# Gate and up as whole 1 MB tiles in the expert steps of four

## Chip, core and metric

The kernel runs on one NeuronCore of a Trainium2 chip. The metric is the device time of one execution in microseconds (us); the median of 3 runs is given. Five engines work side by side: PE (matrix products; its weight loads are listed as PEld), DVE, ACT and POOL (element-wise work), and SP, which here issues nearly all DMAs.

## What is computed

Two pre-norm residual layers on 256 tokens of 1024 channels, all in float32. Layer 0 mixes tokens with a Conformer convolution module, layer 1 with causal differential attention. Each mixer is followed by a mixture of experts, then by a gated per-layer embedding; a final RMSNorm ends the trunk. The part that matters here is the mixture: 32 experts in 4 groups of 8, each token going to one group and to 2 experts in it.

```python
D_MODEL, SEQ, DEPTH = 1024, 256, 2
N_GROUPS, EXPERTS_PER_GROUP, TOP_K_IN_GROUP = 4, 8, 2
D_EXPERT = 256
...
    for g in range(N_GROUPS):
        hg = jnp.einsum("bsd,edf->bsef", h, w_gate[g])
        ug = jnp.einsum("bsd,edf->bsef", h, w_up[g])
        act = jax.nn.silu(hg) * ug * combine[:, :, g, :, None]
        out = out + jnp.einsum("bsef,efd->bsd", act, w_down[g])
```

An expert has three matrices of 1 MB: gate and up are 1024 x 256, down is 256 x 1024. Both layers read all 32 experts, so 192 MB of expert weights pass through the core in one execution.

## The kernel before

Weights go through a ring of 16 slots of 1 MB in SBUF. The class `Stream` holds a list of tiles in the order of their use; `fill` (line 204) takes the next ones, gives each a slot and has SP issue its loads. A slot is freed when `done` (line 233) is called for its tile, and `done` calls `fill` again. The list is therefore the order of the DMA queue: `add_experts` (line 269) writes it for the experts.

A mixture runs in steps, by the table `STEPS` (line 31). Layer 0 has 8 steps of four experts with 32 token slots each. Layer 1 sorts its experts by their counts of tokens: 8 steps of two experts (64 slots each; one of these steps is cut differently) and then 4 steps, 8 to 11, of four experts with 32 slots. In layer 1 the matrices of all places but the first six are found at run time, through `load_found` (line 260).

In every step `add_experts` lists, for `c4` = 0 and 1, one tile per expert that holds half of gate and half of up: of the 8 rows of 256 that each of the 128 partitions owns, four of gate and four of up. Two loads of 512 KB fill it, each 4 KB per partition. After the tiles of both halves come the down tiles, one load of 1 MB each, 8 KB per partition. Three tiles of the first step of each layer (`EARLY`) are loaded ahead into buffers of their own.

The work of a step u in `moe` (line 1024) is, in this order on PE: `gate_up(u, 0, 4)` and `gate_up(u, 4, 8)` (line 1129), `slots(u)` and the token dispatch of a later step, `combine` of the step before, `turn(u)`, and `down(u)` (line 1162). In `gate_up` the tokens of an expert (`hg`) are the stationary operand and the weights stream through:

```python
for c in range(c0, c1):
    for e, s0, width, at in columns(steps[u]):
        ...
        nc.tensor.matmul(ps[at:at + width], hg[:, c, s1:s1 + width], w[:, :, c % 4],
```

With 32 slots per expert, four experts write the four quarters of one PSUM bank: columns 0 to 255 are gate, 256 to 511 are up, and one matmul of 512 columns makes both for one of the 8 rows. PE asks for the four tiles of a half one after the other. `finish_up` (line 1144) turns gate and up into the activation, and after `down(u)` the step's four down slots are freed.

Loads wait at SP in two ways: for the last reader of the slot, and for the semaphore that the load uses. Eight such semaphores go round (DMAHW0 to DMAHW7 in the rows of order below).

Of the kernel before, what the change touches and what calls it, by code (L numbers as in the profile page):

```python
# [32 lines left out]
         + [[(6, 0, 32), (6, 32, 32), (6, 64, 32), (31, 0, 32)]]  # L33
         + [[(7 + 2 * u, 0, 64), (8 + 2 * u, 0, 64)] for u in range(4)]
         + [[(15 + 4 * u + h, 0, 32) for h in range(4)] for u in range(4)])
LAYOUTS = ((0, 32, 64, 96), (0, 64), (0, 96))
CAP = 32
RING = 16
# [51 lines left out]
def kernel(  # L90
# [158 lines left out]
    def places(step):  # L249
        return list(dict.fromkeys(part[0] for part in step))  # L250
# [3 lines left out]
    def expert(e):  # L254

        if e not in order:
            order[e] = nc.sync.value_load(order["row"][0:1, e:e + 1], min_val=0, max_val=NE - 1)
        return bass.ds(order[e] + NE, 1)

    def load_found(t, e, c4):  # L260
        if c4 is None:
            w = moe_w_down.rearrange("l g e f d -> (l g e) f d")[expert(e)]
            nc.sync.dma_start(t, w.rearrange("o (p c) n -> p (o c) n", c=2))
            return
        for m, w in enumerate((moe_w_gate, moe_w_up)):
            w = w.rearrange("l g e d f -> (l g e) d f")[expert(e)].rearrange("o (p c) f -> p (o c) f", c=8)
            nc.sync.dma_start(t[:, 4 * m:4 * m + 4], w[:, 4 * c4:4 * c4 + 4])

    def add_experts(i):
        for u, step in enumerate(STEPS[i]):  # L270
            for c4 in range(2):
                for e in places(step):
                    b = (i * NE + e) * D * F + c4 * 4 * F
                    key = ("gu", i, e, c4)
                    src = [dram(w, b, [[8 * F, P], [F, 4], [1, F]]) for w in (moe_w_gate, moe_w_up)]
                    if i and e >= FIXED:
                        if W.held is None:
                            W.held = len(W.src)
                        src = lambda t, e=e, c4=c4: load_found(t, e, c4)
                    if key[2:] in EARLY[i]:  # L280
                        W.early[key] = src
                    else:
                        W.add(key, src, (8, F))
            if u == PROJ_AT[i]:
                W.add(("proj", i), dram(ple_w_proj, i * 256 * D, [[2 * D, P], [D, 2], [1, D]]), (2, D))
            for e in places(step):
                b = (i * NE + e) * D * F
                src = dram(moe_w_down, b, [[2 * D, P], [D, 2], [1, D]])
                if i and e >= FIXED:
                    src = lambda t, e=e: load_found(t, e, None)  # L290
                W.add(("down", i, e), src, (2, D))

    for jj in range(4):
# [730 lines left out]
    def moe(i, R, between):  # L1024
# [4 lines left out]
        with ExitStack() as ctx:  # L1029
# [99 lines left out]
            def gate_up(u, c0, c1):  # L1129
                hg = hgs[u // 2]  # L1130
                if c0 == 0:
                    gus[u] = ps_a()
                ps = gus[u]
                for c in range(c0, c1):
                    for e, s0, width, at in columns(steps[u]):
                        s1 = (u % 2) * P + at
                        w = W.get("gu", i, e, c // 4).rearrange("p (s c) f -> p s c f", s=2)
                        nc.tensor.matmul(ps[at:at + width], hg[:, c, s1:s1 + width], w[:, :, c % 4],  # L1138
                                         start=(c == 0), stop=(c == 7))
                    if c % 4 == 3:  # L1140
                        for e in places(steps[u]):
                            W.done("gu", i, e, c // 4)

            def finish_up(u):
                ps = gus.pop(u)
# [812 lines left out]
```

## Time and profile before

| | |
|---|---|
| median of 3 runs | 816.93 us (814.59 to 819.43) |
| profiled execution | 815.6 us |
| its span, first to last instruction | 813.9 us |
| PE busy | 699.6 us (86%) |
| PE weight loads busy | 423.5 us (52%) |
| DVE, ACT, POOL busy | 389.4, 297.8, 128.6 us |
| DMA | 246.29 MB in 76112 packets, mean 303 GB/s |
| gate and up matmuls, line 1138 | 191.5 us busy, 50.1 us idle before |
| down matmuls, line 1170 | 82.1 us busy, 9.5 us idle before |

The span is one execution on the chip, as the hardware profiler took it. Busy time is the union of an engine's instructions; a busy PE need not run at its peak. "Idle before" is the time in which the engine waited in front of such an instruction. The DMA share is the mean busy share of the 16 DMA engines of the core and can come out slightly over 1. PE's granted clock has two levels, 1.2 and 2.4 GHz; the page gives it as a share of the higher.

### The profile page before, as it was taken

The numbers are of one execution on the slowest core, as the hardware profiler recorded it, in microseconds if no ns is written. First come the engines' busy times: TensorE is split into PE (matmuls) and PEld (weight loads), VectorE is DVE, ScalarE is ACT, GpSimd is POOL, SyncE is SP. The second block draws the span as 40 slices with busy tenths as digits, with TensorE's granted clock in tenths as the row PEclk, the third lists the DMA queues.
The fourth block names the chain that finished last, engine by engine and source line by source line (L and its number), as shares of the span: only waits on it lengthen the run. The fifth ranks groups of instructions, "written<-read, shape, count | busy, mean of one in ns | idle before, by whom it ended". The sixth has DMA issues, their size and how long they took to land.

```text
span 813.9 us, 11540 instructions
## 1 busy us (share of the span) xinstructions
PE 699.6 (86%) x4038; PEld 423.5 (52%) x4038; DVE 389.4 (48%) x1018; ACT 297.8 (37%) x668; POOL 128.6 (16%) x195
## 2 busy tenths in 40 slices
PE   5999968897786778779999898988999999877796
PEld 3788656643331333225898786764445444422255
DVE  3699975622220521217767886572334324202174
ACT  1577723521110212007656666452212212210064
POOL 1487862000000000001013342100000000000011
PEclk9899989999998989879999999997999999999899
DMA  6990365789999999999854128672899999999951
GB/s 186 337 395 9 89 270 166 282 331 405 411 416 413 409 415 410 413 400 376 264 185 155 54 104 307 249 272 104 332 404 397 412 412 411 412 410 413 416 205 52
DMA packets 76112, 246.29 MB, mean 303 GB/s; under 512 B 8626, under 2 KB 29811, under 8 KB 67602
## 3 DMA queue, kind: packets, MB, share of 16 engines
q1 hardware_dynamic: 75906, 245.24, 78.7%
q8 instruction: 34, 0.56, 0.3%
q10 hardware_dynamic: 144, 0.26, 0.1%
q14 instruction: 28, 0.23, 0.1%
HBM read 244.43 MB, written 1.05 MB: 302 GB/s over the span
## 4 chain that ended last, share of the span: by engine, by line
PE 27%; DMA 12%; DVE 7%; ACT 5%; issue 1%; SPq 0%; POOL 0%; POOLq 0%; ACTq 0%; DVEq 0%
PE psa L1138 7%; DMA wslot<-in_moe_w_up_dram 5%; PE psd L1170 4%; DMA wslot<-in_moe_w_down_dram 4%; PE psb L1076 3%; DMA wslot<-in_ple_w_gate_dram 2%; PE psa L430 2%; DVE wslot L189 2%; PE psa L431 2%; PE psa L432 2%; PE psd L1184 2%; DMA wslot<-in_moe_w_gate_dram 1%; ACT e L1649 1%; ACT wslot L173 1%; PE psc L431 1%
## 5 line engine op out<-in xcount | busy, mean ns | idle before, releaser
L1138 PE MATMUL psa<-wslot,hg 128*32 128x512 f32 (+1 forms) x1008 | 191.5, 675 | 50.1 <-DMA wslot<-in_moe_w_up_dram 49.7
L1138 PEld LDWEIGHTS psa<-wslot,hg 128*32 128x32 f32 (+1 forms) x1008 | 52.5, 127 | 180.1 <-issue 164.2
L1120 DVE TENSOR_REDUCE wc<-psb 32x1 f32<-32x2 f32 (+1 forms) x66 | 10.3, 156 | 208.4 <-PE psb L1115 207.7
L1170 PE MATMUL psd<-wslot,aT 128*32 128x512 f32 (+1 forms) x528 | 82.1, 604 | 9.5 <-DVEq L1404 2.8
L1147 ACT ACTIVATE sg<-psa 128x256 f32<-128x256 f32 x20 | 7.7, 385 | 208.7 <-PE psa L1138 208.7
L1174 DVE TENSOR_TENSOR dl<-psd,dh 128x512 fp32r<-128x512 f32 x40 | 27.6, 692 | 88.4 <-ACT dh L1173 88.4
L872 PE MATMUL psa<-hT,wslot 128*128 128x256 f32 x256 | 58.6, 388 | 1.7 <-DVE hT L761 1.7
L1187 DVE TENSOR_TENSOR x<-x,psd 128x512 f32<-128x512 f32 x80 | 50.0, 683 | 16.1 <-PE psd L1184 16.1
L872 PEld LDWEIGHTS psa<-hT,wslot 128*128 128x128 f32 x256 | 49.7, 195 | 9.3 <-DVE hT L761 2.2
L1170 PEld LDWEIGHTS psd<-wslot,aT 128*32 128x32 f32 (+1 forms) x528 | 21.5, 117 | 59.8 <-issue 45.3
L1173 ACT ACTIVATE dh<-psd 128x512 fp32r<-128x512 f32 x40 | 23.8, 597 | 78.4 <-PE psd L1170 78.4
L387 POOL TENSOR_SCALAR rstd<-ss 128x1 f32<-128x1 f32 x7 | 3.0, 424 | 294.8 <-ACT sq L394 293.9
L821 DVE SCALAR_TENSOR_TENSOR chain<-vp,wT,chain 128x256 f32<-128x256 f32 x119 | 48.0, 483 | 0.2
L1076 PE MATMUL psb<-S,xh 128*128 128x256 f32 x144 | 40.0, 310 | 4.5 <-DVE st L1126 2.2
L430 PE MATMUL psa<-wslot,hTa 128*128 128x256 f32 x144 | 43.5, 302 | 0.0
L1081 ACT ACTIVATE hg<-psb,gains 128x256 f32<-128x256 f32 x72 | 30.3, 471 | 33.5 <-PE psb L1076 33.3
L431 PE MATMUL psa<-wslot,hTa 128*128 128x256 f32 x144 | 41.4, 287 | 0.0
L432 PE MATMUL psa<-wslot,hTa 128*128 128x256 f32 x144 | 41.3, 287 | 0.0
L796 ACT ACTIVATE prod<-vp,wT 128x256 f32<-128x256 f32 x83 | 35.9, 498 | 12.6 <-POOL vp L786 6.8
L1076 PE MATMUL psb<-S,xl 128*128 128x256 f32 x144 | 36.7, 287 | 0.0
L801 POOL TENSOR_TENSOR part<-part,prod 128x256 f32<-128x256 f32 x51 | 35.4, 735 | 0.0
L189 DVE TENSOR_TENSOR wslot<-wslot 128x512 fp32r<-128x512 f32 x39 | 33.4, 885 | 2.7 <-ACT wslot L188 2.7
(344 smaller groups left out, 1340.8 us busy)
## 6 DMA issues: line engine op xcount, KB each, us to landing
wslot<-in_moe_w_down_dram SPq DMA_DIRECT2D x64, 1024.0 KB
wslot<-in_moe_w_gate_dram SPq DMA_DIRECT2D x122, 512.0 KB
wslot<-in_moe_w_up_dram SPq DMA_DIRECT2D x122, 512.0 KB
wslot<-in_conv_w_pw_dram SPq DMA_DIRECT2D x12, 1024.0 KB
wslot<-in_da_w_qkv_dram SPq DMA_DIRECT2D x12, 1024.0 KB
wslot<-in_ple_w_gate_dram SPq DMA_DIRECT2D x8, 1024.0 KB
wslot<-in_da_w_o_dram SPq DMA_DIRECT2D x4, 1024.0 KB
early<-in_moe_w_gate_dram SPq DMA_DIRECT2D x6, 512.0 KB
```

The costliest lines, as they stand in the source:

```text
L189: eng.tensor_tensor(lo, w, hi.bitcast(F32), op=ALU.subtract)
L430: nc.tensor.matmul(ps, h[:, 0, c], wh, start=first, stop=False)
L431: nc.tensor.matmul(ps, h[:, 0, c], wl, start=False, stop=False)
L432: nc.tensor.matmul(ps, h[:, 1, c], wh, start=False, stop=last)
L796: nc.scalar.activation(pr, vps[j][:, k:k + T], AF.Copy, scale=wT[:, j, k:k + 1])
L801: nc.gpsimd.tensor_tensor(part[:, n % 2], part[:, n % 2], pr, op=ALU.add)
L821: nc.vector.scalar_tensor_tensor(pc[n], vps[j][:, k:k + T], wT[:, j, k:k + 1], pe if start else pc[n], op0=ALU.mult, op1=ALU.add)
L872: nc.tensor.matmul(pws[j][:, (1 - half) * T:(2 - half) * T], W.get("pw1", j // 2, 1 - half)[:, c, j % 2 * P:(j % 2 + 1) * P], hT[:, c], st ...
L1076: nc.tensor.matmul(ps[:, c * 256:(c + 1) * 256], xx[tt][:, cc], S[:, tt], start=(n == 0), stop=(n == 3))
L1138: nc.tensor.matmul(ps[at:at + width], hg[:, c, s1:s1 + width], w[:, :, c % 4], start=(c == 0), stop=(c == 7))
L1170: nc.tensor.matmul(pd[at:at + w], aT[:, c, at:at + w], W.get("down", i, e)[:, c, k * 512:(k + 1) * 512], start=(c == 0), stop=(c == 1))
L1187: nc.vector.tensor_add(x[:, tt, ks], x[:, tt, ks], ps)
```

## The change

A table `WHOLE = (1, 8)` names for each layer the first step that is done the new way: steps 1 to 7 of layer 0 and 8 to 11 of layer 1, the steps of four experts but for the first of layer 0. In these, `add_experts` lists the four gate matrices of the step as tiles of their own and then the four up matrices, each with one load of 1 MB that takes 8 KB per partition. `gate_up` reads gate in its first half and up in its second: for all 8 rows and four experts a matmul of 256 columns, into the left and then the right half of the same PSUM bank. `load_found` now takes the list of matrices and the first row. The other steps keep their tiles, loads and matmuls.

```diff
--- before.py
+++ after.py
@@ -33,6 +33,8 @@
          + [[(6, 0, 32), (6, 32, 32), (6, 64, 32), (31, 0, 32)]]
          + [[(7 + 2 * u, 0, 64), (8 + 2 * u, 0, 64)] for u in range(4)]
          + [[(15 + 4 * u + h, 0, 32) for h in range(4)] for u in range(4)])
+
+WHOLE = (1, 8)
 LAYOUTS = ((0, 32, 64, 96), (0, 64), (0, 96))
 CAP = 32
 RING = 16
@@ -257,37 +259,38 @@
             order[e] = nc.sync.value_load(order["row"][0:1, e:e + 1], min_val=0, max_val=NE - 1)
         return bass.ds(order[e] + NE, 1)
 
-    def load_found(t, e, c4):
-        if c4 is None:
-            w = moe_w_down.rearrange("l g e f d -> (l g e) f d")[expert(e)]
-            nc.sync.dma_start(t, w.rearrange("o (p c) n -> p (o c) n", c=2))
-            return
-        for m, w in enumerate((moe_w_gate, moe_w_up)):
-            w = w.rearrange("l g e d f -> (l g e) d f")[expert(e)].rearrange("o (p c) f -> p (o c) f", c=8)
-            nc.sync.dma_start(t[:, 4 * m:4 * m + 4], w[:, 4 * c4:4 * c4 + 4])
+    def load_found(t, e, ws, c0=0):
+        n = t.shape[1] // len(ws)
+        for m, w in enumerate(ws):
+            w = w.rearrange("l g e a b -> (l g e) a b")[expert(e)]
+            w = w.rearrange("o (p c) n -> p (o c) n", c=2 if ws == (moe_w_down,) else 8)
+            nc.sync.dma_start(t[:, m * n:(m + 1) * n], w[:, c0:c0 + n])
 
     def add_experts(i):
         for u, step in enumerate(STEPS[i]):
-            for c4 in range(2):
-                for e in places(step):
-                    b = (i * NE + e) * D * F + c4 * 4 * F
-                    key = ("gu", i, e, c4)
-                    src = [dram(w, b, [[8 * F, P], [F, 4], [1, F]]) for w in (moe_w_gate, moe_w_up)]
-                    if i and e >= FIXED:
-                        if W.held is None:
-                            W.held = len(W.src)
-                        src = lambda t, e=e, c4=c4: load_found(t, e, c4)
-                    if key[2:] in EARLY[i]:
-                        W.early[key] = src
-                    else:
-                        W.add(key, src, (8, F))
+
+            parts = [((w,), 0) for w in (moe_w_gate, moe_w_up)]
+            if u < WHOLE[i]:
+                parts = [((moe_w_gate, moe_w_up), 4 * c4) for c4 in range(2)]
+            for n, e in [(n, e) for n in range(2) for e in places(step)]:
+                ws, c0 = parts[n]
+                b = (i * NE + e) * D * F + c0 * F
+                src = [dram(w, b, [[8 * F, P], [F, 8 // len(ws)], [1, F]]) for w in ws]
+                if i and e >= FIXED:
+                    if W.held is None:
+                        W.held = len(W.src)
+                    src = lambda t, e=e, ws=ws, c0=c0: load_found(t, e, ws, c0)
+                if u == 0 and (e, n) in EARLY[i]:
+                    W.early["gu", i, e, n] = src
+                else:
+                    W.add(("gu", i, e, n), src, (8, F))
             if u == PROJ_AT[i]:
                 W.add(("proj", i), dram(ple_w_proj, i * 256 * D, [[2 * D, P], [D, 2], [1, D]]), (2, D))
             for e in places(step):
                 b = (i * NE + e) * D * F
                 src = dram(moe_w_down, b, [[2 * D, P], [D, 2], [1, D]])
                 if i and e >= FIXED:
-                    src = lambda t, e=e: load_found(t, e, None)
+                    src = lambda t, e=e: load_found(t, e, (moe_w_down,))
                 W.add(("down", i, e), src, (2, D))
 
     for jj in range(4):
@@ -1131,15 +1134,19 @@
                 if c0 == 0:
                     gus[u] = ps_a()
                 ps = gus[u]
-                for c in range(c0, c1):
-                    for e, s0, width, at in columns(steps[u]):
-                        s1 = (u % 2) * P + at
-                        w = W.get("gu", i, e, c // 4).rearrange("p (s c) f -> p s c f", s=2)
-                        nc.tensor.matmul(ps[at:at + width], hg[:, c, s1:s1 + width], w[:, :, c % 4],
-                                         start=(c == 0), stop=(c == 7))
-                    if c % 4 == 3:
-                        for e in places(steps[u]):
-                            W.done("gu", i, e, c // 4)
+                whole = u >= WHOLE[i]
+                for n in range(c0 // 4, c1 // 4):
+                    for c in range(8) if whole else range(4 * n, 4 * n + 4):
+                        for e, s0, width, at in columns(steps[u]):
+                            s1 = (u % 2) * P + at
+                            w, out = W.get("gu", i, e, n), ps[at:at + width]
+                            if whole:
+                                w, out = w[:, c], out[:, n * F:(n + 1) * F]
+                            else:
+                                w = w.rearrange("p (s c) f -> p s c f", s=2)[:, :, c % 4]
+                            nc.tensor.matmul(out, hg[:, c, s1:s1 + width], w, start=(c == 0), stop=(c == 7))
+                    for e in places(steps[u]):
+                        W.done("gu", i, e, n)
 
             def finish_up(u):
                 ps = gus.pop(u)
```

Two engines show what is issued now. PE in step 1 of layer 0, before (psa is the PSUM bank, wslot the ring, hg the tokens; a wait names the semaphore of a load):

```order
L1138 MATMUL psa<-wslot,hg 32x512 [waits DMAHW6_49,DMAHW5_49]
L1138 MATMUL psa<-wslot,hg 32x512 [waits DMAHW7_49,DMAHW0_49]
L1138 MATMUL psa<-wslot,hg 32x512 [waits DMAHW2_49,DMAHW1_49]
L1138 MATMUL psa<-wslot,hg 32x512 [waits DMAHW4_49,DMAHW3_49]
L1138 MATMUL psa<-wslot,hg 32x512 x12
L1138 MATMUL psa<-wslot,hg 32x512 [waits DMAHW6_49,DMAHW5_49]
L1138 MATMUL psa<-wslot,hg 32x512 [waits DMAHW7_49,DMAHW0_49]
L1138 MATMUL psa<-wslot,hg 32x512 [waits DMAHW2_49,DMAHW1_49]
L1138 MATMUL psa<-wslot,hg 32x512 [waits DMAHW4_49,DMAHW3_49]
L1138 MATMUL psa<-wslot,hg 32x512 x12
L1111 MATMUL psb<-wgt_hl,S 128x8 x2
```

and with the change, where each half has four matmuls that wait for one load each, and 28 more of 256 columns:

```order
L1147 MATMUL psa<-wslot,hg 32x256 [waits DMAHW5_49]
L1147 MATMUL psa<-wslot,hg 32x256 [waits DMAHW6_49]
L1147 MATMUL psa<-wslot,hg 32x256 [waits DMAHW7_49]
L1147 MATMUL psa<-wslot,hg 32x256 [waits DMAHW0_49]
L1147 MATMUL psa<-wslot,hg 32x256 x28
L1147 MATMUL psa<-wslot,hg 32x256 [waits DMAHW1_49]
L1147 MATMUL psa<-wslot,hg 32x256 [waits DMAHW2_49]
L1147 MATMUL psa<-wslot,hg 32x256 [waits DMAHW3_49]
L1147 MATMUL psa<-wslot,hg 32x256 [waits DMAHW4_49]
L1147 MATMUL psa<-wslot,hg 32x256 x28
L1114 MATMUL psb<-wgt_hl,S 128x8 x2
```

The first of the half's matmuls for each expert waited for two loads and now waits for one; 12 that follow became 28, half as wide. What stands behind them on PE is the same.

SP in the second half of the same step and its down tiles, before:

```order
L215 DMA wslot<-in_moe_w_gate_dram 128x1024 [waits DMAHW5_49,PE_49]
L215 DMA wslot<-in_moe_w_up_dram 128x1024 [waits DMAHW6_49]
L215 DMA wslot<-in_moe_w_gate_dram 128x1024 [waits DMAHW7_49,PE_49]
L215 DMA wslot<-in_moe_w_up_dram 128x1024 [waits DMAHW0_49]
L215 DMA wslot<-in_moe_w_gate_dram 128x1024 [waits DMAHW1_49,PE_49]
L215 DMA wslot<-in_moe_w_up_dram 128x1024 [waits DMAHW2_49]
L215 DMA wslot<-in_moe_w_gate_dram 128x1024 [waits DMAHW3_49,PE_49]
L215 DMA wslot<-in_moe_w_up_dram 128x1024 [waits DMAHW4_49]
L217 DMA wslot<-in_moe_w_down_dram 128x2048 [waits DMAHW5_49,PE_49]
L217 DMA wslot<-in_moe_w_down_dram 128x2048 [waits DMAHW6_49,PE_49]
L217 DMA wslot<-in_moe_w_down_dram 128x2048 [waits DMAHW7_49,PE_49]
L217 DMA wslot<-in_moe_w_down_dram 128x2048 [waits DMAHW0_49,PE_49]
```

and with the change:

```order
L217 DMA wslot<-in_moe_w_up_dram 128x2048 [waits DMAHW1_49,PE_49]
L217 DMA wslot<-in_moe_w_up_dram 128x2048 [waits DMAHW2_49,PE_49]
L217 DMA wslot<-in_moe_w_up_dram 128x2048 [waits DMAHW3_49,PE_49]
L217 DMA wslot<-in_moe_w_up_dram 128x2048 [waits DMAHW4_49,PE_49]
L219 DMA wslot<-in_moe_w_down_dram 128x2048 [waits DMAHW5_49,PE_49]
L219 DMA wslot<-in_moe_w_down_dram 128x2048 [waits DMAHW6_49,PE_49]
L219 DMA wslot<-in_moe_w_down_dram 128x2048 [waits DMAHW7_49,PE_49]
L219 DMA wslot<-in_moe_w_down_dram 128x2048 [waits DMAHW0_49,PE_49]
```

Eight loads of 128x1024 elements became four of 128x2048, which is the shape that the down loads have, and every load now waits for the slot's last reader itself.

## Rows read from the trace of the kernel before

**Rows 1.** Page, part 2: bytes moved in 40 slices, and the packets.

```profile
GB/s 186 337 395 9 89 270 166 282 331 405 411 416 413 409 415 410 413 400 376 264 185 155 54 104 307 249 272 104 332 404 397 412 412 411 412 410 413 416 205 52
DMA packets 76112, 246.29 MB, mean 303 GB/s; under 512 B 8626, under 2 KB 29811, under 8 KB 67602
```

**Rows 2.** Stretches by stage: us, busy (instructions) by engine, PE clock, DMA share, GB/s.

```profile
174.00:184.00 10.00, 9.76 (x91) 4.12 (x84) 2.84 (x10) 1.82 (x4) 0.00 (x0) 1.00 0.77 244
184.00:214.00 30.00, 25.41 (x171) 10.99 (x173) 8.38 (x18) 5.47 (x12) 0.00 (x0) 0.94 1.02 413
...
640.00:683.00 43.00, 43.00 (x241) 20.85 (x245) 16.50 (x34) 10.80 (x24) 0.00 (x0) 1.00 1.02 413
...
723.00:782.00 59.00, 43.04 (x233) 14.09 (x234) 13.38 (x29) 6.06 (x11) 0.00 (x0) 0.91 1.01 410
```

**Rows 3.** Waits of PE (184:372, then 678:779): us, times, longest.

```profile
PE psa L1138 <- DMA wslot<-in_moe_w_up_dram: 37.5, 27, 1.6
...
PE psa L1138 <- DMA wslot<-in_moe_w_up_dram: 12.3, 9, 1.5
```

**Rows 4.** Timeline of PE, layer 1: step 10, and the end of step 11.

```profile
723.14 3.63 PE L1138 MATMUL psa<-wslot,hg 128*32 128x512 f32 x28 [0.46 <-DMA wslot<-in_moe_w_up_dram]
...
764.62 3.59 PE L1138 MATMUL psa<-wslot,hg 128*32 128x512 f32 x26 [1.53 <-DMA wslot<-in_moe_w_up_dram]
...
774.50 3.62 PE L1170 MATMUL psd<-wslot,aT 128*32 128x512 f32 x26 [1.46 <-DMA wslot<-in_moe_w_down_dram]
```

**Rows 5.** Page, part 6: loads of expert weights, count and KB each.

```profile
wslot<-in_moe_w_down_dram SPq DMA_DIRECT2D x64, 1024.0 KB
wslot<-in_moe_w_gate_dram SPq DMA_DIRECT2D x122, 512.0 KB
```

**Rows 6.** Timeline of PE, layer 0, step 4: start, us, what.

```profile
247.39 1.02 PE L1138 MATMUL psa<-wslot,hg 128*32 128x512 f32 x2 [1.53 <-DMA wslot<-in_moe_w_up_dram]
249.94 1.02 PE L1138 MATMUL psa<-wslot,hg 128*32 128x512 f32 x2 [1.53 <-DMA wslot<-in_moe_w_up_dram]
```

**Rows 7.** Stretches with gate and up loads alone (columns of Rows 2).

```profile
212.00:227.00 15.00, 10.55 (x58) 2.47 (x52) 1.45 (x3) 1.19 (x2) 0.00 (x0) 0.80 1.03 409
...
306.00:321.00 15.00, 14.96 (x82) 5.73 (x82) 1.62 (x3) 3.85 (x7) 0.00 (x0) 1.00 1.03 408
```

**Rows 8.** Stretches with down loads alone (columns of Rows 2).

```profile
201.00:207.00 6.00, 6.00 (x36) 1.92 (x33) 0.39 (x3) 0.38 (x1) 0.00 (x0) 0.75 1.02 423
232.00:238.00 6.00, 5.44 (x41) 2.64 (x42) 1.44 (x7) 0.78 (x3) 0.00 (x0) 1.00 1.02 424
...
327.00:332.00 5.00, 4.66 (x26) 1.26 (x26) 0.00 (x0) 0.00 (x0) 0.00 (x0) 0.68 1.01 419
357.00:361.00 4.00, 3.24 (x16) 0.92 (x20) 0.00 (x0) 0.00 (x0) 0.00 (x0) 0.57 1.01 418
```

**Rows 9.** Timeline of PE, layer 0: step 1, and the end of step 7.

```profile
174.39 7.05 PE L1138 MATMUL psa<-wslot,hg 128*32 128x512 f32 x64
...
357.76 5.18 PE L1138 MATMUL psa<-wslot,hg 128*32 128x512 f32 x26 [1.51 <-DMA wslot<-in_moe_w_up_dram]
```

**Rows 10.** Stretches where layer 1's queue fills again (columns of Rows 2).

```profile
572.00:578.00 6.00, 6.00 (x30) 1.95 (x26) 0.34 (x1) 0.12 (x1) 0.00 (x0) 1.00 0.80 283
578.00:584.00 6.00, 6.00 (x38) 4.32 (x39) 4.34 (x10) 2.33 (x6) 0.00 (x0) 1.00 1.02 424
```

**Rows 11.** Chain of waits: start, us, what (a load, issue to landing).

```profile
744.04 10.22 DMA wslot<-in_moe_w_up_dram
```

**Rows 12.** Timeline of PE's weight loads: step 3, and the end of step 7.

```profile
233.17 0.16 PEld L1138 LDWEIGHTS psa<-wslot,hg 128*32 128x32 f32 x4 [0.27 <-issue]
233.60 0.16 PEld L1138 LDWEIGHTS psa<-wslot,hg 128*32 128x32 f32 x4 [0.27 <-issue]
...
367.72 0.16 PEld L1170 LDWEIGHTS psd<-wslot,aT 128*32 128x32 f32 x8 [0.99 <-DMA wslot<-in_moe_w_down_dram]
```

**Rows 13.** Groups by line: busy us, mean ns of one (convolution).

```profile
L872 PE MATMUL psa<-hT,wslot 128*128 128x256 f32 x256 | 58.6, 388 | 1.7 <-DVE hT L761 1.7
```

## The prediction

> **What bounds the kernel now.** I read the slices of the span first. The moved bytes stand at 400 GB/s and more in two long stretches, and mostly far lower elsewhere [rows 1]. The stage table puts numbers on that: from 184 us on (layer 0's experts) and from 640 to 782 us (layer 1's) the 16 DMA engines are busy all the time (share 1.01 to 1.02) at 410 to 413 GB/s, while PE has gaps [rows 2]. So in both stretches the weights come as fast as the DMA engines carry them, and PE waits: 37.5 us for up tiles between 184 and 372 us, 12.3 us between 678 and 779 us [rows 3]. Up to 723 us PE in layer 1 runs without such a wait (the one of 0.46 us there is the first [rows 4]); that does not contradict it, since the DMA engines are full at the same time, and it is they that are still behind when PE has caught up.
>
> Next, what the engines carry. The issue part of the page has 64 down loads of 1 MB and 122 gate loads of 512 KB [rows 5]; beside each gate load stands one of up. A down load takes 8 KB from one place for each of 128 partitions, a half gate or up load 4 KB. The packet line says the same: 76112 packets, 67602 of them under 8 KB, and the remaining 8510 are close to 66 x 128 = 8448, the down loads and the two of the projection [rows 1]. So one row is one packet, and the trace already holds both sizes.
>
> Do they run at different speeds? I picked stretches in which only one kind is in flight. Where PE is released by one up tile after another, 2.55 us apart, it is gate and up, as from 247.39 to 249.94 us [rows 6]. The ten microseconds after a step's last up tile are down. Two stretches of the first kind ran at 409 and 408 GB/s, mean 408.5 [rows 7]; four of the second at 418 to 424, mean 421 [rows 8]. The DMA share is full in all six. A tile of 1 MB so costs 1048.6/408.5 = 2.567 us in 4 KB rows and 1048.6/421 = 2.491 us in 8 KB rows: **0.076 us less**. From the slower end of one to the slower end of the other (409 to 418) it is 0.055, from 408 to 424 it is 0.097.
>
> **The change, part by part.** *Loads.* Seven steps of layer 0 (1 to 7) and four of layer 1 (8 to 11) load eight 1 MB tiles of one matrix each, so 88 tiles go from two loads with 4 KB rows to one with 8 KB rows, the shape of the down loads. The bytes and the order (8 tiles, then 4 down) stay.
> - Step 1 of layer 0, 8 tiles: worth nothing. PE ran its gate and up at 174.39 us in one piece of 64 records (the trace has two for a matmul) without a wait [rows 9]; the tiles had been there.
> - Steps 2 to 7, 48 tiles: 48 x 0.076 = 3.6 us (2.6 to 4.7).
> - Layer 1, 32 tiles: 32 x 0.076 = 2.4 us. The first eight travel while PE still works without waiting [rows 4]; if they only come earlier into slots that PE frees no sooner, 24 count: 1.8 us. Ends 1.3 and 3.1.
> - The start of step 2. Between 174 and 184 us, where the queue fills again, 4 KB rows ran at only 244 GB/s [rows 2]. Layer 1 has the same: 283 GB/s from 572 to 578 us on 4 KB rows, then 424 as soon as 8 KB rows follow [rows 10]. Were step 2's tiles at 421 here, 10 x (1 - 244/421) = 4.2 us would be gained; if the slowness belongs to the filling of the queue, nothing. No row shows 8 KB rows in those first microseconds, so I take a quarter, 1.0 us.
>
> *SP.* 88 issues go. SP is not what is waited for, since it runs ahead: a load issued at 744.04 us took 10.22 us to land [rows 11], four tiles of 2.55 us, so eight loads are in flight. With 1 MB each that is 8 MB and some 20 us ahead. The ring has 16 slots and PE holds the four of the current half, so slots suffice, and what stands behind (routing inputs, projection, gate weights of the stage after) keeps its place in bytes. Zero.
>
> *PE.* 32 more matmuls in each of the 11 steps, each 256 columns wide, so the columns stay and the weight loads double. Now four loads of 32 columns stand together every 0.43 us (233.17, 233.60) and take 0.16 us [rows 12]; they hide behind the 512 columns of the four matmuls. With 256 columns the four have 0.215 us, so 0.16 still fits if it may overlap. The nearest row for that width is the convolution's: 256 records of 128x256 with 128-wide weights in 58.6 us busy, 0.229 each [rows 13]. I take that: 16 x 0.229 = 3.7 us for a half of a step against 8 x 0.43 = 3.4 now. The lower end is 0.215 (no loss), the upper 0.215 + 0.16 = 0.375, load and columns one after the other. A third of a microsecond per half is covered wherever PE waits, 1.5 us at nearly every tile [rows 6]. Uncovered is only the last half before a stage ends, where the down loads of 10 us follow. There PE got the last up tile of layer 0 at 357.76 us [rows 9], and its weight loads for down then waited 0.99 us for a tile [rows 12]; in layer 1 it waited 1.46 us [rows 4]. The extra fits into both waits: zero. If the cover were gone it would cost 0.3 us at each.
>
> The clock bears on this tail: the 26 records after 357.76 us took 5.18 us, the same 26 after 764.62 us only 3.59 [rows 4, 9]. From 357 to 361 us the mean granted clock was 0.57 [rows 8], mostly the lower level of 1.2 GHz, after a half in which PE had waited at nearly every tile. A layer-0 tail at 2.4 GHz would widen the cover; I count neither.
>
> *Sum:* 3.6 + 2.4 + 1.0 = **7.0 us** off the profiled execution's 815.6 us (span 813.9), giving 808.6. That execution lies 1.3 us under the median of the runs, 816.93, so the forecast for the median is **809.9 us**.
>
> The Trainium skill has a rule that speaks against the PE term. "TensorE: Matmul & The Clock Gate", Part 3, The mechanism, says that weight loads overlap matmuls in flight only when their row group differs. All four tiles here use all 128 rows, so by it nothing would overlap, neither now nor later. The trace does not agree: with loads of 0.16 us behind 0.43 us of columns the four come every 0.43 us, not every 0.59 [rows 12]. By the rule the sum would be that of rival 1.
>
> **Rivals.**
> 1. *The weight loads come into the open (slower).* With half the columns behind them the four loads might no longer hide, and four matmuls take 0.375 us instead of 0.215: a half needs 6.0 us, 2.6 more than now. In layer 1 that is 8 x 2.6 = 20.8 us of PE work against 12.3 + 1.5 = 13.8 us of waits [rows 3, 4], so PE becomes the bound there: +7. Layer 0 (14 halves, 36.4 us against waits of 37.5) keeps some of its 3.6 us, less the tail, where 2.6 meets a cover of 0.99: -2. Together +5, **822 us**. It decides from about 0.30 us for four on: 8 x 16 x (0.30 - 0.215) = 10.9 us, about what the saving of 2.4 us leaves of layer 1's waits. For it: twice the loads. Against it: the 0.229 us of the convolution with loads four times as wide [rows 13]. Chance 0.07.
> 2. *The rate does not follow the row (no change).* The difference of 3% might belong to something else that the down loads have, and both sizes be full speed: then 816.9. Against it: the six stretches, all with full engines, fall into two groups that do not overlap [rows 7, 8]. Chance 0.14, with the case that the loads are cut into 4 KB pieces after all, against which the 8510 packets speak. The Trainium skill's page "DMA: Bandwidth & Descriptors", Specifications, has that rule: line rate from 512 bytes on. By it both sizes are at line rate and the forecast would be no change.
> 3. *Layer 1 keeps nothing.* PE works without waiting for tiles until 723 us [rows 4]; if slots, freed at PE's pace, hold the loads back, only layer 0's 3.6 us remain: **813.3 us**. Against it: the engines are full from 640 us on [rows 2], so the slots were there. Chance 0.11.
> 4. *The start gives all of its 4.2 us*: 3.2 more than forecast, **806.7 us**. For it: 8 KB rows at 424 right behind the slow stretch [rows 10]. Chance 0.08.
>
> **How the numbers follow.** The forecast, a saving of 4.5 to 9 us, has 0.60. A measurement of this kernel can tell about 0.5%, 4 us, from no change. Faster by more than that: forecast and rival 4, 0.68. Within it: rivals 2 and 3, 0.25. Slower: rival 1, 0.07. The terms' ends give 2.6 + 1.3 = 3.9 us to 4.7 + 3.1 + 4.2 = 12.0 us, 813.0 to 804.9; for 8 in 10 I take 805.5 at the low side and reach over rival 3 towards rival 2 at the high one, 816.0. The repeated runs of the kernel before spread over 814.59 to 819.43, which is why neither end is drawn closer.
>
> **What would show it.** Right: between 184 and 360 us the rate is 418 to 424 GB/s throughout, no longer in two levels; the packets under 8 KB fall by 88 x 256 = 22528 and those of 8 KB rise by 11264; layer 0's experts end 3 to 5 us earlier, and the last down tile of layer 1 comes 6 us or more before 774.50 us [rows 4]. Gate and up records come in groups of four every 0.22 to 0.24 us, and PE still waits for DMA at the up and gate tiles. Wrong: a rate that stays at 409 GB/s on gate and up (rival 2); groups of four at 0.30 us or more and DMA waits of PE gone (rival 1); DMA share under 1 between 660 and 720 us (rival 3).

## Result and the profile after

The changed kernel takes **809.36 us** (median of 4 runs, 808.37 to 810.18) beside 818.18 us for the kernel before on the same chip (4 runs, 814.59 to 819.97): a ratio of 0.9897, 95% interval 0.9859 to 0.9936, some 8.4 us less. A second comparison gave 809.18 us and 0.9902 (0.9882 to 0.9921). The profiled execution took 810.18 us (span 808.5), 5.4 us less than the profiled one of before, which lay low in its own scatter. The forecast was 809.9 us, a saving of 7.0 us; the median lies nearer to it than the saving does, because the kernel before came out at 818.18 us here and at 816.93 in the three runs that the forecast started from.

The page of the changed kernel, parts 2 and 6, answers to [rows 1, 5]:

```profile
GB/s 175 322 408 30 53 263 187 285 359 422 420 420 421 418 417 421 420 399 366 265 157 157 53 105 313 251 270 104 343 391 407 410 418 421 415 420 421 417 191 52
DMA packets 63444, 246.36 MB, mean 305 GB/s; under 512 B 7218, under 2 KB 28403, under 8 KB 43666
...
wslot<-in_moe_w_down_dram SPq DMA_DIRECT2D x64, 1024.0 KB
wslot<-in_moe_w_gate_dram SPq DMA_DIRECT2D x44, 1024.0 KB
...
wslot<-in_moe_w_gate_dram SPq DMA_DIRECT2D x34, 512.0 KB
```

The packets of 8 KB went from 76112 - 67602 = 8510 to 63444 - 43666 = 19778, by 11268 (88 tiles x 128 rows = 11264). Those under 8 KB fell by 23936, which is 1408 more than the 88 x 256 of the prediction: packets under 512 B fell by 1408 as well, 16 for each of the 88 loads that are gone. The slices of the expert stages went from 400 to 416 GB/s to as much as 422.

Stretches by stage and stretches with gate and up loads alone, changed kernel (us, busy and instructions by engine, PE clock, DMA share, GB/s), which answer to [rows 2, 7]:

```profile
174.00:184.00 10.00, 9.92 (x158) 5.70 (x148) 2.47 (x8) 1.32 (x4) 0.00 (x0) 1.00 0.78 301
184.00:214.00 30.00, 25.74 (x245) 13.95 (x246) 9.82 (x22) 6.86 (x15) 0.00 (x0) 0.94 1.02 422
...
640.00:683.00 43.00, 43.00 (x315) 21.15 (x314) 14.25 (x31) 8.99 (x20) 0.00 (x0) 1.00 1.01 419
...
723.00:777.00 54.00, 39.13 (x303) 17.47 (x301) 13.51 (x28) 6.46 (x12) 0.00 (x0) 0.84 1.00 410
...
212.00:222.00 10.00, 6.04 (x50) 2.17 (x46) 1.38 (x2) 0.60 (x1) 0.00 (x0) 0.73 1.02 420
306.00:316.00 10.00, 8.79 (x101) 3.33 (x99) 1.38 (x2) 1.86 (x4) 0.00 (x0) 1.00 1.01 420
```

Gate and up alone now run at 420 GB/s, where they ran at 408 to 409 [rows 7], and the ten microseconds at the start of step 2 went from 244 to 301 GB/s. From 723 us on the rate stayed at 410: the last load ends inside that window.

PE's waits in the two stages (184 to 372 us, then 678 to 779 us: us, times, longest), to [rows 3]:

```profile
PE psa L1147 <- DMA wslot<-in_moe_w_up_dram: 24.1, 14, 2.5
PE psa L1147 <- DMA wslot<-in_moe_w_gate_dram: 16.3, 11, 1.9
...
PE psa L1147 <- DMA wslot<-in_moe_w_up_dram: 8.7, 5, 2.2
PE psa L1147 <- DMA wslot<-in_moe_w_gate_dram: 6.4, 4, 2.5
```

PE waits longer for gate and up together than it did for up, 40.4 us where it was 37.5 and 15.1 where it was 12.3; so it still waits for loads in both stages.

And PE's timeline (start, us): step 7 of layer 0 with its down and the first work of the per-layer embedding; the first half of step 10 in layer 1; the end of step 11. To [rows 4, 9]:

```profile
352.88 5.33 PE L1147 MATMUL psa<-wslot,hg 128*32 128x256 f32 x58 [1.86 <-DMA wslot<-in_moe_w_up_dram]
...
361.85 4.75 PE L1177 MATMUL psd<-wslot,aT 128*32 128x512 f32 x32
...
717.80 3.65 PE L1147 MATMUL psa<-wslot,hg 128*32 128x256 f32 x60 [0.60 <-DMA wslot<-in_moe_w_gate_dram]
...
756.63 0.62 PE L1147 MATMUL psa<-wslot,hg 128*32 128x256 f32 x2 [1.87 <-DMA wslot<-in_moe_w_up_dram]
759.12 5.33 PE L1147 MATMUL psa<-wslot,hg 128*32 128x256 f32 x58 [1.87 <-DMA wslot<-in_moe_w_up_dram]
...
768.09 4.62 PE L1177 MATMUL psd<-wslot,aT 128*32 128x512 f32 x32
```

The last up tile of layer 0 came 4.9 us earlier than before (357.76), that of layer 1 5.5 us earlier (764.62). So layer 0 carries most of the gain. Both last halves took 5.33 us here, and down did not wait for a tile; before, the last 26 of down's 32 records in layer 1 waited until 774.50 us [rows 4].

### The profile page after: what moved, and what is told of

It reads as the page before. It is cut to its first block, busy times and chain, and to the rows that moved or that the text cites. A ratio compares the mean times of both kernels' runs of the same rounds, so it can differ in the third digit from the quotient of the medians.

```text
span 808.5 us, 12701 instructions
## 1 busy us (share of the span) xinstructions
PE 692.8 (86%) x4742; PEld 451.2 (56%) x4742; DVE 390.0 (48%) x1018; ACT 297.5 (37%) x668; POOL 128.1 (16%) x195
## 2 busy tenths in 40 slices
DMA packets 63444, 246.36 MB, mean 305 GB/s; under 512 B 7218, under 2 KB 28403, under 8 KB 43666
## 5 line engine op out<-in xcount | busy, mean ns | idle before, releaser
L1147 PE MATMUL psa<-wslot,hg 128*32 128x256 f32 (+2 forms) x1712 | 181.6, 478 | 56.0 <-DMA wslot<-in_moe_w_up_dram 32.8
L1147 PEld LDWEIGHTS psa<-wslot,hg 128*32 128x32 f32 (+1 forms) x1712 | 77.7, 129 | 157.8 <-issue 61.2
L875 PE MATMUL psa<-hT,wslot 128*128 128x256 f32 x256 | 61.0, 399 | 2.4 <-DMA wslot<-in_conv_w_pw_dram 2.4
L433 PE MATMUL psa<-wslot,hTa 128*128 128x256 f32 x144 | 42.8, 297 | 0.0
L435 PE MATMUL psa<-wslot,hTa 128*128 128x256 f32 x144 | 40.6, 282 | 0.0
L434 PE MATMUL psa<-wslot,hTa 128*128 128x256 f32 x144 | 40.6, 282 | 0.0
```

Source lines behind the costliest of these rows:

```text
L433: nc.tensor.matmul(ps, h[:, 0, c], wh, start=first, stop=False)
L434: nc.tensor.matmul(ps, h[:, 0, c], wl, start=False, stop=False)
L435: nc.tensor.matmul(ps, h[:, 1, c], wh, start=False, stop=last)
L875: nc.tensor.matmul(pws[j][:, (1 - half) * T:(2 - half) * T], W.get("pw1", j // 2, 1 - half)[:, c, j % 2 * P:(j % 2 + 1) * P], hT[:, c], st ...
L1147: nc.tensor.matmul(out, hg[:, c, s1:s1 + width], w, start=(c == 0), stop=(c == 7))
```

## Experiments

In the table, "ple 0" is the start of the per-layer embedding behind layer 0's experts in the profiled execution (PE's first product of its gate weights), "ple 0 to 1" the time from there to the same point of layer 1; the first shows what layer 0 gained, the second what layer 1 gained. Both come from one execution for each kernel: six that do layer 0 as the changed kernel does have ple 0 at 369.45 to 370.72 us, so a difference of 1 us in these columns can be scatter. Ratios are to the kernel before, run beside it on the same chip.

| kernel | median us | ratio, 95% interval | ple 0 | ple 0 to 1 |
|---|---|---|---|---|
| before (median of the first 3 runs) | 816.93 | | 375.46 | 406.78 |
| changed | 809.36 | 0.9897 (0.9859 to 0.9936) | 370.72 | 406.11 |
| changed, again | 809.18 | 0.9902 (0.9882 to 0.9921) | 370.21 | 405.60 |
| layer 0 alone | 811.98 | 0.9943 (0.9926 to 0.9961) | 370.61 | 407.40 |
| layer 1 alone | 814.99 | 0.9981 (0.9965 to 0.9998) | 375.90 | 407.06 |
| two loads a tile | 816.16 | 0.9983 (0.9968 to 0.9999) | 375.55 | 407.51 |
| one load, 4 KB | 815.80 | 0.9987 (0.9969 to 1.0004) | 374.37 | 408.58 |
| one load, 2 KB | 828.15 | 1.0134 (1.0112 to 1.0155) | 382.00 | 414.03 |
| split matmuls | 817.99 | 1.0015 (0.9998 to 1.0031) | 378.35 | 408.98 |
| layer 0 from step 3 | 812.24 | 0.9943 (0.9924 to 0.9962) | 373.21 | 405.72 |
| all of layer 1 | 809.17 | 0.9899 (0.9881 to 0.9917) | 370.26 | 405.51 |
| layer 1, last two | 811.24 | 0.9934 (0.9916 to 0.9952) | 369.79 | 405.66 |
| layer 1, first two | 810.26 | 0.9919 (0.9890 to 0.9949) | 369.45 | 407.72 |
| end by expert | 809.58 | 0.9906 (0.9887 to 0.9925) | 370.56 | 405.39 |

The changed kernel once more, unedited, beside the runs on 4 KB rows in one load, on all of layer 1 and on the end by expert:

> The changed kernel once more, beside the runs below. Both theories: 7 to 9 us less than before; layer 0's and layer 1's parts measured alone (4.7 and 1.5 us by medians) and the 0.6 us that the changed kernel with 4 KB rows kept let one expect 6.5 to 8. If the two layers' gains did not add up (layer 1 gaining only because layer 0 leaves it another clock), over 9 or under 6.

8.0 us less than before (6.5 to 9.6), where the two layers alone give 4.7 + 1.6 = 6.3: within their intervals the gains add up, though the sum by itself lies just under this one.

### Each layer alone

```diff
-WHOLE = (1, 8)
+WHOLE = (1, 12)
```

> Layer 0's steps 1 to 7 read whole tiles of one matrix, layer 1 is as before. Row theory (the gain comes from 8 KB rows, tile by tile): layer 0 keeps what it gained in the profile of the changed kernel, where its last half ended 4.7 us earlier than before: 4 to 6 us less than the kernel before, rate 415 to 422 GB/s between 184 and 334 us, and layer 1 as before at 410 to 413. Order theory (PE gains because gate is finished before up, whatever the loads): also a gain, but the rate between 184 and 334 us stays at 409 on gate and up. Rival, both layers are needed because the gain is made at the end of layer 1: within 1.5 us of before.

4.7 us less by the ratio, as the row theory had it, and from 184 to 214 us the rate is 421 GB/s, not the order theory's 409. The third of these expectations (a gain only together) is out.

```diff
-WHOLE = (1, 8)
+WHOLE = (8, 8)
```

> Only layer 1's steps 8 to 11 read whole tiles of one matrix. Row theory with the loads as the limit to the end: 2 to 3 us less than the kernel before. Row theory with PE's clock as the limit at the end (in the changed kernel the last half took 5.3 us for what took 3.6 before, and down waited for no tile any more): 0 to 1.5 us less, the last up tile some 2 us earlier, and the last half again over 4.5 us long with no wait of down behind it. Weight loads in the open: not less, or more.

1.6 us less (0.2 to 2.9), which does not tell the two versions of the row theory apart. The last half took 5.33 us here too. From ple 0 to 1 the profiled execution shows no gain (407.06 us, before 406.78); it took 816.33 us, more than the median of its runs.

### Row, number of loads, or order of the matmuls

Two loads of 512 KB for each whole tile, in `add_experts` and in the same way in `load_found`:

```diff
-                src = [dram(w, b, [[8 * F, P], [F, 8 // len(ws)], [1, F]]) for w in ws]
+                src = [dram(w, b + h * F, [[8 * F, P], [F, 4], [1, F]])
+                       for w in ws for h in ((0,) if len(ws) == 2 else (0, 4))]
```

> The changed kernel's tiles, order and matmuls, but each whole tile comes in two loads of 512 KB with 4 KB rows. Row theory: the gain is gone, within 1.5 us of the kernel before, rate 408 to 410 GB/s on gate and up, 76112 packets again. Order theory: 7 to 9 us less than before, as the changed kernel. Theory of the weight loads as a hidden loss: slower than before by what they cost.

One load, in pieces of 4 KB and then of 2 KB (shown is the side of the memory; the side of the tile and `load_found` are cut into the same pieces):

```diff
-                src = [dram(w, b, [[8 * F, P], [F, 8 // len(ws)], [1, F]]) for w in ws]
+                src = [dram(w, b, [[8 * F, P], [F, 4], [1, F]]) for w in ws]
+                if len(ws) == 1:
+                    src = [dram(ws[0], b, [[4 * F, P], [512 * F, 2], [1, 4 * F]])]
...
+                    src = [dram(ws[0], b, [[2 * F, P], [256 * F, 4], [1, 2 * F]])]
```

> The changed kernel with the same number of loads, one of 1 MB for each whole tile, but each partition gets its 8 KB as two pieces of 4 KB from places 512 KB apart (the channels of a weight tile are so no longer those of its input: the experts' results are not the reference's). Row theory: like the changed kernel with two loads, within 2 us of before, rate 408 to 414 GB/s on gate and up, 76112 packets. Theory that the number of load instructions decides: 7 to 9 us less than before, rate 418 to 422. For the start of step 2: if fewer loads alone fill the queue faster, 300 GB/s between 174 and 184 us as in the changed kernel; if the row does it, 240 to 270.

> As the run with one load in two pieces of 4 KB, now with four pieces of 2 KB from places 256 KB apart (the experts' results are again not the reference's). Theory of a fixed cost for each row: the two measured rates, 421 GB/s at 8 KB and 408.5 at 4 KB, give 0.3113 and 0.1604 us for a row on one of 16 engines, so 0.0095 us fixed, 0.0850 us for 2 KB and 385 GB/s; a tile of 1 MB takes 2.72 us, 0.23 more than now; 48 tiles of layer 0 lose 11 us and 20 to 32 of layer 1 lose 5 to 7: 824 to 828 us, 7 to 11 over the kernel before, and 385 GB/s where gate and up travel alone. Rival (a threshold between 4 and 8 KB, all smaller rows alike): 409 GB/s and 815 to 817 us. If a row of 2 KB costs as much as one of 4 KB: about half the rate.

With 4 KB rows, in two loads or in one, nearly all of the gain is gone (1.4 and 1.1 us are left, with intervals that reach to 0.1 and to -0.3). The order and the matmuls of both are those of the changed kernel, so the order does not make the gain, and neither does the number of loads by itself. The changed kernel, beside the run with one load of 4 KB rows on the same chip, is 6.6 us faster (809.18 and 815.80, ratios 0.9902 and 0.9987 with intervals apart); between these two only the pieces of a load differ. Gate and up loads alone in the three kernels, columns as above; two loads a tile:

```profile
212.00:222.00 10.00, 6.13 (x52) 2.01 (x46) 1.38 (x2) 1.19 (x2) 0.00 (x0) 0.82 1.03 409
308.00:318.00 10.00, 10.00 (x105) 4.68 (x103) 1.38 (x2) 2.39 (x4) 0.00 (x0) 1.00 1.03 412
```

One load, 4 KB:

```profile
212.00:222.00 10.00, 5.96 (x46) 1.87 (x42) 1.38 (x2) 1.19 (x2) 0.00 (x0) 0.74 1.02 407
308.00:318.00 10.00, 9.37 (x103) 3.58 (x101) 1.39 (x2) 2.39 (x4) 0.00 (x0) 1.00 1.03 410
```

One load, 2 KB, three stretches:

```profile
218.00:228.00 10.00, 6.32 (x64) 2.88 (x64) 0.00 (x0) 0.00 (x0) 0.00 (x0) 0.66 1.05 387
310.00:320.00 10.00, 9.91 (x52) 3.46 (x50) 0.69 (x1) 3.36 (x6) 0.00 (x0) 1.00 1.05 387
344.00:354.00 10.00, 4.29 (x28) 1.30 (x24) 1.38 (x2) 1.20 (x2) 0.00 (x0) 0.80 1.05 387
```

387 GB/s with 2 KB rows, where a fixed cost for each row had given 385 beforehand and a threshold 409. So the rate follows the row: 387, 407 to 412, 418 to 424 [rows 7, 8] GB/s for 2, 4 and 8 KB, as if each row cost about 0.01 us beside its bytes. The traces also hold the time of each packet, and it agrees: from 186 to 345 us the median packet took 0.088 us at 2 KB and 0.164 at 4 KB (the two runs with one load) and 0.312 at 8 KB (changed kernel), so twice the shorter packet takes 0.012 and 0.016 us more than the longer one. The time of 828.15 us is at the upper end of what was expected.

### The price of the weight loads

```diff
+                    split = u >= (1, 8)[i] and 0 < c < 7
+                    for m in range(2 if split else 1):
...
+                            if split:
+                                w, out = w[:, m], out[:, m * F:(m + 1) * F]
```

> The kernel before with its loads, but in the 11 steps the matmuls of channels 1 to 6 are each split in two of 256 columns (so six of eight groups have twice the weight loads). Row theory, with weight loads that hide: within 1.5 us of before, groups of four 256-column matmuls every 0.22 to 0.24 us. Weight loads in the open (0.375 us for four): 3 us or more slower. Order theory says nothing here (the order of gate and up is as before): 0.

1.2 us slower, interval 0.2 us faster to 2.5 slower: not the 3 us of weight loads in the open, but a small cost is not excluded. The profiled execution, the slowest of twelve (820.72 us), is 2.9 us later at ple 0 and 2.2 us longer from there to ple 1. In the changed kernel itself 60 records from 717.80 us took 3.65 us, 0.243 for four, just above the 0.22 to 0.24 looked for.

### The start of step 2

```diff
-WHOLE = (1, 8)
+WHOLE = (3, 8)
```

> The changed kernel, but in layer 0 the steps 1 and 2 keep half tiles as before; steps 3 to 7 and layer 1 are changed. Theory that the start of step 2 gains by the number of loads (one of 1 MB in place of two of 512 KB): between 174 and 184 us the rate falls back from 301 to 321 GB/s to about 241, which is 1.4 to 1.9 us, and eight tiles lose 0.076 each, 0.6 us: 2.0 to 2.5 us slower than the changed kernel, 5.5 to 6 less than before. Theory that what is won at the start is lost behind it (slots and PE set the pace of step 2): within 1 us of the changed kernel.

2.9 and 3.1 us slower than the changed kernel by the medians, 2.5 and 3.0 by ple 0 (373.21 to 370.72 and 370.21). The rates at the start of step 2 (columns as above) bear on why. Changed from step 3 on only:

```profile
174.00:184.00 10.00, 9.76 (x88) 4.48 (x81) 2.86 (x9) 1.88 (x5) 0.00 (x0) 1.00 0.85 241
...
178.00:180.00 2.00, 2.00 (x24) 0.65 (x20) 0.00 (x0) 0.00 (x0) 0.00 (x0) 1.00 0.96 315
180.00:182.00 2.00, 2.00 (x20) 1.12 (x13) 0.56 (x4) 0.38 (x1) 0.00 (x0) 1.00 0.98 184
182.00:184.00 2.00, 1.76 (x15) 1.54 (x14) 1.61 (x5) 0.90 (x3) 0.00 (x0) 1.00 0.93 287
```

One load of 1 MB, but with 4 KB rows:

```profile
174.00:184.00 10.00, 10.00 (x158) 5.80 (x150) 2.36 (x7) 1.39 (x3) 0.00 (x0) 1.00 0.81 297
...
178.00:180.00 2.00, 2.00 (x44) 1.17 (x36) 0.00 (x0) 0.00 (x0) 0.00 (x0) 1.00 1.01 416
180.00:182.00 2.00, 2.00 (x44) 1.17 (x36) 0.00 (x0) 0.00 (x0) 0.00 (x0) 1.00 1.03 424
182.00:184.00 2.00, 2.00 (x22) 1.39 (x14) 0.97 (x5) 0.38 (x1) 0.00 (x0) 1.00 1.01 408
```

The changed kernel's second execution:

```profile
174.00:184.00 10.00, 9.77 (x153) 5.97 (x146) 2.80 (x9) 1.56 (x4) 0.00 (x0) 1.00 0.82 321
```

With half tiles, two loads each, the engines are busy (share 0.93 to 0.98) and carry 184 to 315 GB/s; with one load of the same rows they carry 408 to 424 from 178 us on. So most of this part of the gain does not need the longer row. How much of it is the number of loads and how much the order of the tiles is not separated: two loads of one matrix, in the new order, were in between at 269 GB/s, and the run with 4 KB rows, at 297, is at the low end of the changed kernel's 301 and 321. What in many small loads slows the engines there, and no longer from 186 us on, these runs do not show.

### Which tiles of layer 1 count

```diff
-WHOLE = (1, 8)
+WHOLE = (1, 1)
```

> Whole tiles of one matrix also in steps 1 to 7 of layer 1, 16 more expert loads. Row theory with the DMA as the limit to layer 1's end: 16 x 2 x 0.076 = 2.4 us less than the changed kernel. If slots that PE frees no sooner, or PE's clock at the end, set layer 1's end: within 1 us of the changed kernel. Weight loads in the open in steps of two experts (64 columns each, no cover by waits there): slower than the changed kernel.

Steps 1 to 7 hold 14 experts, so it was 28 tiles and at 0.076 us each 2.1 us, not the 2.4 expected. They bring nothing: 809.17 beside 809.18 us. SP's issues of down loads in layer 1's steps of two experts say why; the kernel before:

```profile
574.40 1.23 SPq L263 DMA_DIRECT2D wslot<-in_moe_w_down_dram  x2
...
636.38 0.92 SPq L263 DMA_DIRECT2D wslot<-in_moe_w_down_dram  x2
```

Whole tiles in all of layer 1:

```profile
570.08 0.95 SPq L267 DMA_DIRECT2D wslot<-in_moe_w_down_dram  x2
...
632.19 0.91 SPq L267 DMA_DIRECT2D wslot<-in_moe_w_down_dram  x2
```

Four steps take 61.98 us with 4 KB rows and 62.11 with 8 KB. The loads go at the pace at which PE frees slots; in the kernel before PE is busy 69.75 of the 70 us from 570 to 640, at a DMA share of 0.97:

```profile
570.00:640.00 70.00, 69.75 (x404) 31.74 (x400) 23.05 (x48) 15.31 (x34) 0.00 (x0) 1.00 0.97 383
```

The changed kernel, and then whole tiles in all of layer 1:

```profile
570.00:640.00 70.00, 69.75 (x410) 33.98 (x407) 24.64 (x54) 16.86 (x38) 0.00 (x0) 1.00 1.01 399
```

```profile
570.00:640.00 70.00, 69.75 (x587) 44.11 (x584) 24.84 (x54) 17.01 (x38) 0.00 (x0) 1.00 0.98 400
```

PE's 69.75 us are the same in all three. So a nearly full DMA share does not mean that the DMA sets the pace. Two more runs ask the same of steps 8 to 11, the second with a range of steps in place of the first step:

```diff
-WHOLE = (1, 8)
+WHOLE = (1, 10)
...
+WHOLE = ((1, 8), (8, 10))
```

> In layer 1 only the last two steps read whole tiles of one matrix (16 expert tiles), layer 0 as in the changed kernel. Theory that layer 1's loads are paced by the slots that PE frees up to about 700 us, so that only later tiles count: within 0.7 us of the changed kernel, and the time from the first layer-1 load behind 565 us to the last up tile is as in the changed kernel, 187.8 to 188.7 us. Theory that all 32 tiles count: 1.2 us more, 189 to 190 us.

> The complement of the run before: in layer 1 only steps 8 and 9 read whole tiles of one matrix, steps 10 and 11 halves as before; layer 0 as in the changed kernel. Theory that layer 1's loads are paced by the slots that PE frees up to about 700 us: the 16 tiles of steps 8 and 9 bring nothing, the time is that of the run with layer 0 alone, 811 to 813 us, and the last up tile comes 189.5 us or more behind the first down load after 565 us. Theory that all 32 tiles count: half of layer 1's gain, 0.8 to 1.6 us less than with layer 0 alone, 810 to 811 us. If steps 8 and 9 carry the gain and the last two nothing, as the times (not the trace) of the run before would have it: 809 to 810 us.

The profiled executions fit the theory: from ple 0 to ple 1 the last two steps alone take 405.66 us, as the changed kernel (405.60, 406.11), and the first two alone 407.72, as with layer 0 alone (407.40). From the first down load behind 565 us to the last up tile it was 188.63 and 189.75 us, where the theory had said 187.8 to 188.7 and 189.5 or more. The measured times lean the other way (5.4 and 6.6 us less than before), with intervals that overlap each other and those of both theories. **Inconclusive** for steps 8 and 9; for the steps of two experts it is settled.

### The end of the layers

The last step takes its experts one, one, and two together:

```diff
+                cols = columns(steps[u])
+                groups = (cols[0:1], cols[1:2], cols[2:4]) if u == ns - 1 else (cols,)
```

> The changed kernel, but in the last step of each layer gate and up are computed expert by expert as the tiles come, the last two together (cover of four experts at once given up). Theory that PE at the lower clock ate layer 1's gain at the end: the work behind the last up tile falls from 5.3 to 1.8 to 3.4 us, down then waits for its tiles again (0.5 us or more) and each layer ends 0.3 to 2 us earlier: 0.5 to 3 us less than the changed kernel. If the end is set by the down tiles or by what follows them anyway: within 0.5 us of the changed kernel. If the extra PE work (four times 1.7 us in place of 3.7) is in the way: slower.

No gain: 0.9906 beside 0.9902. The end of layer 1 in this run:

```profile
758.24 3.64 PE L1149 MATMUL psa<-wslot,hg 128*32 128x256 f32 x30 [1.06 <-DMA wslot<-in_moe_w_up_dram]
...
768.21 3.62 PE L1179 MATMUL psd<-wslot,aT 128*32 128x512 f32 x26 [1.46 <-DMA wslot<-in_moe_w_down_dram]
```

The work behind the last up tile is down to 3.64 us, but what it saves down gives back in a wait of 1.46 us. Down's second piece begins at 768.21 us and takes 3.62; in the changed kernel, with the slow last half, down ran from 768.09 for 4.62 us. So, by these two executions, the slower last half costs layer 1 about 0.9 us at most.

## Why the prediction was right, and where not

- **Rates by row** (421 against 408.5 GB/s): held, 420 and 407 to 412. Rival 2 is out. The page "DMA: Bandwidth & Descriptors" of the Trainium skill gives line rate from 512 bytes on in Specifications; the measurement decides against it here, at 387, 409 and 421 GB/s. The Trainium skill's page "DMA: Bandwidth & Descriptors", section "Why small descriptors are slow (HBM only)", names a fixed overhead for each packet, with 256 bytes as its example. The kind of cost agrees with what is seen here at 2 to 8 KB.
- **Layer 0's tiles, 3.6 us for 48:** held or a little less. Layer 0's gain to ple 0 is 4.7 and 5.3 us (375.46 to 370.72 and 370.21). Steps 1 and 2 make 2.5 to 3.0 of it, so the 40 tiles of steps 3 to 7 make some 2.25 us, 0.056 each where 0.076 was taken and 0.055 was the lower end. That rests on one execution of each kernel, with a scatter of about 1 us; the rates of 408.5 and 420 GB/s give 0.070 for a tile, so it is not shown that the term was too large.
- **The start of step 2, 1.0 of 0 to 4.2 us:** too small, if anything. Steps 1 and 2 together are worth 2.5 to 3.0 us; less step 2's 8 tiles at 0.056 to 0.076, about 2 to 2.5 us belong to the start. Two other readings are lower: the bytes (301 or 321 for 244 GB/s over 10 us) come to 1.4 to 1.8 us at 421 GB/s, and the run with one load and 4 KB rows, which has the start without the longer rows, was only 1.1 us earlier at ple 0 (374.37). So the start gave 1.1 to 2.5 us. The guess that 8 KB rows make it was wrong in the main: one load with 4 KB rows gives 297 GB/s already, the changed kernel 301 and 321. Rival 4, all of the 4.2 us, did not come either: neither is 421. The pause itself stayed; SP issued the first load of step 2 at 175.36 us, before it had been 174.58:

```profile
160.55 7.19 SPq L219 DMA_DIRECT2D wslot<-in_moe_w_down_dram  x4
175.36 0.80 SPq L217 DMA_DIRECT2D wslot<-in_moe_w_gate_dram  x2
```

- **Layer 1, 2.4 us:** 1.6 us by the run of layer 1 alone (0.2 to 2.9), which does not exclude 2.4. The step that does not hold is the reading of full engines as the limit where PE has no gap. The prediction gave PE gaps in both stretches, but from 640 to 683 us PE was busy for all 43.00 us [rows 2], and in steps 1 to 7 faster loads beside a PE as busy brought nothing. Whether the tiles of steps 8 and 9 were counted wrongly by it stays open. Rival 3 had the mechanism, slots at PE's pace, for the steps of two experts, though not its end: with layer 1 alone some gain is left.
- **PE, zero:** held within the measurement. Four 256-column records take 0.243 us where 0.229 was taken, and PE still waits at gate and up tiles. But the cover at the end, a wait of 0.99 us behind the last half of layer 0 and of 1.46 behind that of layer 1, was gone in the profiled execution: the last half took 5.33 us in both layers. The granted clock in layer 1's stretches there was 0.95, then 0.74:

```profile
752.00:757.00 5.00, 3.13 (x40) 1.30 (x32) 0.00 (x0) 0.00 (x0) 0.00 (x0) 0.95 1.01 421
757.00:762.00 5.00, 3.13 (x34) 1.54 (x36) 0.00 (x0) 0.00 (x0) 0.00 (x0) 0.74 1.01 419
```

  So part of it ran at 1.2 GHz, after PE had waited 1.87 us at each of two tiles and worked 0.62 us in between. It also happens without the change: the kernel before had 5.18 us at the end of layer 0 and 3.59 at that of layer 1 [rows 4, 9], and a second execution of the changed kernel had 3.64 and 4.98 (rows below). But it is more frequent with whole tiles: of the 17 last halves on them, in the profiled executions of the kernels of the table but for the 2 KB rows and the end by expert, 14 took 4.9 us or more; of the five on half tiles, the split matmuls left out, two did.

```profile
352.38 3.64 PE L1147 MATMUL psa<-wslot,hg 128*32 128x256 f32 x58 [1.86 <-DMA wslot<-in_moe_w_up_dram]
...
757.70 4.98 PE L1147 MATMUL psa<-wslot,hg 128*32 128x256 f32 x58 [1.87 <-DMA wslot<-in_moe_w_up_dram]
```

- **Rival 1** (weight loads in the open): out by the 3.65 us for 60 records and by the split matmuls.

The sum was right, but that the median came within 0.6 us is luck: no part is measured to better than about 1 us. Rows were to bring 3.6 + 2.4 = 6.0 us, and 6.6 lie between the run with one load of 4 KB rows and the changed kernel. Part by part, 7.0 were forecast (with 1.0 for the start), and the runs give about 2.7 to 3.4 (48 tiles at 0.056 to 0.070), 1.6 and 1.1 to 2.5, together 5.4 to 7.5. Measured are 8.0 us less in the second comparison (0.9902, 6.5 to 9.6 us), so the parts lie at its lower edge. The 1.1 to 1.4 us that the two runs with 4 KB rows kept include their faster start (269 and 297 GB/s); whether more stands behind the gap stays open.

No run beats the changed kernel by more than its scatter.

## What to carry to other kernels

Where loads set the pace, try longer contiguous rows for each partition (8 KB in place of 4 KB gave 3% of the rate here) and one load in place of two where the queue has to fill anew; price it from the rates of rows that the trace already holds. Full DMA engines alone do not show that loads set the pace: look whether the engine that frees the slots waits, and if it is busy throughout, faster loads there may be worth nothing, as 28 more whole tiles were here.

## Not expected of the hardware

- A row costs about the same fixed time at 2, 4 and 8 KB, some 0.01 us: a guess from two rates (385 GB/s for 2 KB) met the third (387).
- After a pause, half tiles in two loads of 512 KB ran at 184 to 315 GB/s on engines that were 0.93 to 0.98 busy, and one load of 1 MB with rows of the same size at 408 to 424.
- Two experts of 32 slots cost PE as much as four: behind the last up tile, 30 records of two took 3.64 us in the run by expert, and 58 records of four also 3.64 in the second execution of the changed kernel, both at the full clock. That is why the 1.8 us that was expected at best behind the last tile did not come. The stretches, by expert and then changed:

```profile
758.00:762.00 4.00, 3.76 (x32) 1.95 (x32) 0.00 (x0) 0.08 (x1) 0.00 (x0) 1.00 1.02 424
```

```profile
352.00:356.00 4.00, 3.62 (x59) 1.99 (x59) 0.00 (x0) 0.00 (x0) 0.00 (x0) 1.00 1.02 426
```
